# GpSimd's splits in 512 columns, and the state-space output scaled by its root mean square in PSUM

## The chip, the cores and the metric

One core of one Trainium2 chip runs the whole program: one launch, 256 tokens, 32-bit floats in and out. The metric is the device time of one execution in microseconds, as a median over runs. The engines are named as in the profile: PE multiplies matrices (PEld is its loading of weights), DVE is the vector engine, ACT the scalar engine, POOL is GpSimd, SP issues the transfers.

## The reference

Two layers, each an FFN, a mixer and a second FFN, with a root-mean-square norm ahead of and behind each of the three. The first layer's mixer is a hybrid of a convolution and a state-space model, the second's is attention. Only the hybrid is touched here:

```python
def conformer_conv(u, w_dw, b_dw, ln_g, ln_b):
    val, gate = jnp.split(u, 2, axis=-1)
    hid = causal_depthwise_conv(val * jax.nn.sigmoid(gate), w_dw, b_dw)     # 31 taps, 1024 channels
    return jax.nn.silu(layer_norm(hid, ln_g, ln_b))

def mamba2_ssd(z, xbc, dt_raw, ...):
    xbc = jax.nn.silu(causal_depthwise_conv(xbc, conv_w, conv_b))           # 4 taps
    xs, bm, cm = jnp.split(xbc, ...)                                        # 1024, 256, 256 channels
    dt = jax.nn.softplus(dt_raw + dt_bias)
    y = ssd_chunked(xs * dt[..., None], dt * a, bm, cm) + d_skip[:, None] * xs
    y = y.reshape(bsz, seq, 1024) * jax.nn.silu(z)
    return rms_norm(y, norm_g)

def conv_ssd_mixer(u, w_in, ..., w_out):
    conv_in, z, xbc, dt_raw = jnp.split(u @ w_in, [2048, 3072, 4608], axis=-1)
    ya = conformer_conv(conv_in, ...)
    yb = mamba2_ssd(z, xbc, dt_raw, ...)
    return jnp.concatenate([ya, yb], axis=-1) @ w_out
```

`rms_norm` of `yb` multiplies each token's row by one number, `rsqrt(mean(y*y) + 1e-6)`, and each channel by a gain.

## The kernel before

Every product is made in three passes in `f32r`: each operand is the sum of a rounded high part and a low part, and `mm3` adds high x high, high x low and low x high in one PSUM tile. Weights come in units of 1 MB (128 x 2048). `prefetch` loads a unit into a `raw` buffer, ACT copies it to `wh` (the rounding), and then `wl = raw - wh` is made on DVE in pieces of 1024 columns (`PIECE`), or, for the units in `GPSIMD_UNITS`, on POOL in pieces of `POOL_PIECE` columns; ACT copies in the same pieces. There are 4 buffers each of `raw`, `wh` and `wl`, and the loading stands three units ahead of the use.

The units of the hybrid, in the order of use: 33 to 40 the convolution's gate and value columns, 41 and 42 B and C of the state-space model, 43 and 44 its first half of channels (`xbc_pair`), 45 and 46 the first half of the gate z (`gate_z`), 47 and 48 and then 49 and 50 the same for the second half, 51 to 54 the rows of the output projection that meet `yb`, 55 to 58 those that meet `ya`. Everything is recorded through one helper, so that all instructions have line 423, and tile names tell them apart:

- `v`: the four tiles `xs[t][g]` (token tile t of 128 tokens, half g of the channels). They hold x, then x times the skip, then y, then y times silu(z). `y0`, `y1` are the silu(z) of the two token tiles.
- `s<-v,m`, `s<-s,m`, `s<-s,s`, `v<-v,heads`, `v<-v,y` on POOL: x times dt, decays, the skip, the gate.
- `cv`, `t`, `c` on DVE: the 31 taps of the convolution, two chains of additions that end in `cv`; `s<-a,chan,s` and `s<-w,chan,s` are the short convolutions of the state-space part.
- `junk<-v` (ACT) sums squares of y; `m` on DVE adds the halves; `m<-m,mhalf` on POOL is the power -1/2 (`rstd`), and the result for token tile 0 is `m1_13`, for 1 `m1_15`.
- `w<-ident,v` on PE: the transposes of y (`spread`), which ACT and DVE leave as high and low parts in `x` (the tile `ybT`).
- after the last tap: PE transposes the convolution's output, DVE and ACT normalise (`s<-t,m,m`, `s<-s,m,m`), PE transposes back, ACT applies silu (`pt`) and splits into `s` (high), DVE into `s` (low): the operands `yaT` of the last units.
- `a_35`, `a_36` (token tile 0, the two halves of 512 output columns) and `a_37`, `a_38` (token tile 1) are the PSUM tiles in which the output projection is summed: first all of `yb`'s units 51 to 54 for token tile 0, then for 1, then unit 55, then 56 to 58.

What scales y before:

```python
r = self.rstd(ss, EPS)
for g in range(2):
    nc.scalar.activation(xs[t][g], xs[t][g], AF.Copy, scale=r)
```

The order on each engine isn't that of the code: a planner (`schedule`) simulates the recorded operations with a cost for each (`cost`) and hand-over times, and picks for each engine the operation that can start first. A change of a cost or of an operation can thus reorder any engine. Each engine then runs its instructions strictly in that order.

Of the kernel before, what the change touches and what calls it, by code (L numbers as in the profile page):

```python
# [10 lines left out]
F32R = mybir.dt.float32r  # L11
BF16 = mybir.dt.bfloat16
AF = mybir.ActivationFunctionType
# [10 lines left out]
EPS = 1e-6  # L24
# [8 lines left out]
LATE = 800  # L33
PIECE = 1024
FIRST_PIECES = (512, 1024)
POOL_PIECE = 256
ON_POOL = (1, 1, 1)
CONV = 2000
GATE = 200
CONV_INIT = (-500, -100)  # L40
GPSIMD_UNITS = range(38, 56)
SB_BUFS = {"s": 18, "v": 4, "cv": 5, "pt": 4, "sg": 4, "x": 4, "y0": 2, "y1": 2}
PS_BUFS = {"a": 4, "w": 2, "t": 1, "c": 1}
SMALL = {1: 16, 2: 12, 8: 12, 12: 2, 16: 6, 32: 8}
# [391 lines left out]
def cost(op, out):  # L436

    kw = op.kw
    op.table = None
    op.shares_port = False  # L440
    n = out.free_size() if isinstance(out, View) else 0
    if op.engine == "tensor":
        stationary = op.args[1]
        if op.name == "transpose":
            return 109.0, 0.0
        if stationary.ap.dtype == F32R:
            return n / 2.4 + 17.0 if n > 256 else 120.0, 0.0
        return 2 * max(2 * n / 2.4 + 2.5, 112.0), 0.0
    psum = any(isinstance(a, View) and a.buf.kind.psum for a in (*op.args, *kw.values()))
    if op.engine == "scalar":  # L450
        op.table = TABLES.get(op.args[2])
        views = sum(isinstance(kw.get(k), View) for k in ("bias", "scale")) + ("accum_out" in kw)
        return 0.832 * n + (52.0 if psum else 96.0) + 93.0 * views, 0.0
    if op.engine == "gpsimd":
        if op.name == "memset":
            return 100.0, 0.0
        if n == 1:
            return 515.0, 0.0
        return (2.35 if out.ap.dtype == F32R else 1.9) * n + 40.0, 0.0
# [12 lines left out]
    cols = dst.free_size() if isinstance(dst, View) else kw["in_"].free_size()  # L472
    return 475.0, cols * P * 4 / 300.0
# [23 lines left out]
class Kernel:  # L497
# [85 lines left out]
        return r(hi), r(lo)  # L583


    def mm3(self, out, a, b, start, stop):
        mm = self.nc.tensor.matmul
        mm(out, a[0], b[0], start=start, stop=False)
        mm(out, a[0], b[1], start=False, stop=False)
        mm(out, a[1], b[0], start=False, stop=stop)  # L590

    def transposed_tile(self):

# [44 lines left out]
    def acc_pairs(self, acc, lhs, unit, kk, start, stop, halves=(0, 1)):  # L638
        hi, lo = unit
        for hf in halves:  # L640
            c = slice(hf * 512, (hf + 1) * 512)
            self.mm3(acc[hf], lhs, (hi[:, kk, c], lo[:, kk, c]), start, stop)

    def to_transposed(self, src, hi_of, lo_of, n, banks="tc", gain=None):

# [199 lines left out]
    def hybrid(self, xT, done):  # L845
        nc = self.nc
# [13 lines left out]
        dt, a = self.step_sizes(xT)  # L860
# [140 lines left out]
        ybT = self.transposed_tile()  # L1001
        st = [None, None]

        def spread(t):
            self.to_transposed(xs[t], *self.x_out(ybT, t), KB, "ww", gain=chan[:, H_SG : H_SG + KB])

        for t in range(NT):
            if t == 0:
                for g in range(2):
                    lt[1, g] = decays(1, g)  # L1010
            else:
                spread(0)
            ss = self.sm(2)
            for g in range(2):
                hs = slice(8 * g, 8 * g + 8)
                y = xs[t][g]
                py = self.ps([P, 512], "a")
                for hh in range(8):
                    nc.tensor.matmul(py[:, hh * 64 : (hh + 1) * 64], lt[t, g][hh // 4][:, hh % 4, :], xd[t][g][:, hh * 64 : (hh + 1) * 64], start=True, stop=True)
                if t == 0:  # L1020
                    xk = self.slot([P, 512])
                    XK.tensor_tensor(out=heads_view(xk), in0=heads_view(xd[t][g]), in1=by_head(left[:, hs]), op=ALU.mult)
                    pst = self.ps([P, 512], "a")
                    nc.tensor.matmul(pst, b0[:, g, :], xk, start=True, stop=True)
                    st[g] = self.slot([P, 512])
                    nc.scalar.activation(st[g], pst, AF.Copy)
                nc.gpsimd.tensor_tensor(out=heads_view(y), in0=heads_view(y), in1=by_head(self.heads[:, 1, hs]), op=ALU.mult)
                V.tensor_tensor(out=y, in0=y, in1=py, op=ALU.add)
                if t == 1:
                    po = self.ps([P, 512], "a")  # L1030
                    nc.tensor.matmul(po, cT[:, g, P : 2 * P], st[g], start=True, stop=True)
                    V.tensor_tensor(out=heads_view(po), in0=heads_view(po), in1=by_head(grow[:, hs]), op=ALU.mult)
                    V.tensor_tensor(out=y, in0=y, in1=po, op=ALU.add)
                YZ.tensor_tensor(out=y, in0=y, in1=zs[t][g], op=ALU.mult)
                self.sumsq(ss[:, g : g + 1], y, 1 / 32.0)
            r = self.rstd(ss, EPS)
            for g in range(2):
                nc.scalar.activation(xs[t][g], xs[t][g], AF.Copy, scale=r)
        spread(1)


# [28 lines left out]
        def out_unit(src, j, t, unit, start, stop, halves=(0, 1)):  # L1070
            for b in range(2):
                self.acc_pairs(acc[t], src(t, j, b), unit, b, start and b == 0, stop and b == 1, halves)

        for t in range(NT):
            acc[t] = self.acc_tile()
        units = [self.unit(D) for _ in range(4)]
        for t in range(NT):
            for j in range(4):
                out_unit(of_yb, j, t, units[j], j == 0, False)

        unit = self.unit(D)
        for t in range(NT):
            out_unit(of_ya, 0, t, unit, False, False)
        tail = [(j, self.unit(D)) for j in (1, 2, 3)]
        for t in range(NT):
            for j, unit, hf in [(j, unit, hf) for hf in range(2) for j, unit in tail]:
                out_unit(of_ya, j, t, unit, False, j == 3, (hf,))
            done(t, acc[t])

    def load_small(self):  # L1090
# [224 lines left out]
```

## Time and profile before

| | before |
|---|---|
| median of 3 runs | 1132.56 us (1129.19 to 1132.75) |
| profiled execution | 1132.12 us, span 1130.3 us, mean granted clock 0.993 |
| PE busy | 1095.5 us, 97% of the span |
| PEld busy | 919.5 us |
| DVE busy | 738.6 us, 65% |
| ACT busy | 635.2 us, 56% |
| POOL busy | 148.2 us, 13% (200 instructions, nearly all between 205 and 378 us) |

The span runs from the first to the last instruction, and the execution's own time is 1.8 us longer. Times in rows are microseconds from the start of the span. The hybrid lies at about 205 to 397 us. In rows of the timeline, a group stands for several like instructions in a row, and what follows in brackets is how long the engine was idle before it and which engine's work ended that. PEclk is the clock that PE was granted, as a share of full speed.

### The profile page before, as it was taken

To read this page: it belongs to the slowest core of one execution; us is meant where nothing else is said; L and a number is where in the kernel's file an instruction comes from. 1 tells how busy PE (TensorE), PEld (TensorE's weight loads), DVE (VectorE), ACT (ScalarE), POOL (GpSimd) and SP (SyncE) were. 2 spreads that over 40 slices of the span, in tenths; PEclk is the share of its full clock that TensorE was granted. 3 is DMA by queue.
4 is the path that set the end of the run, shared out by engine and by line. 5 is a ranking of instruction groups with operands and counts; after the bars stand their busy time and mean duration, and the time that the engine had idled before them with its cause. 6 is when DMAs were issued, how large, how long until landed. Compare 5 with 4: busy or idle time off the path is not lost.

```text
span 1130.3 us, 15336 instructions
## 1 busy us (share of the span) xinstructions
PE 1095.5 (97%) x5830; PEld 919.5 (81%) x5830; DVE 738.6 (65%) x1248; ACT 635.2 (56%) x1217; POOL 148.2 (13%) x200
## 2 busy tenths in 40 slices
PE   6999999999899999999999999999999999999997
PEld 5888888798767778888878888888877877888885
DVE  5756556799797685655686555667575657555563
ACT  7645545788667564554565454545565456455452
POOL 0000000379795300000010000001000000000000
PEclk9999999999999999999999999999999999999999
DMA  9755454534333466546546546554632424654521
GB/s 349 260 189 186 165 208 149 190 146 150 112 109 116 186 229 217 186 157 215 186 149 224 205 174 221 180 193 159 237 138 79 150 75 152 220 181 174 215 83 38
DMA packets 30203, 196.55 MB, mean 174 GB/s; under 512 B 3633, under 2 KB 4529, under 8 KB 7601
## 3 DMA queue, kind: packets, MB, share of 16 engines
q1 hardware_dynamic: 30128, 195.57, 48.9%
q8 instruction: 45, 0.74, 0.2%
q14 instruction: 30, 0.24, 0.1%
HBM read 194.51 MB, written 1.05 MB: 173 GB/s over the span
## 4 chain that ended last, share of the span: by engine, by line
PE 63%; DVE 4%; ACT 3%; POOL 3%; issue 1%; DVEq 0%; POOLq 0%; ACTq 0%
PE w L423 26%; PE a L423 22%; PE t L423 8%; PE c L423 7%; ACT s L423 1%; POOL wl L423 1%; ACT wh L423 1%; DVE y L423 1%; POOL s L423 1%; DVE wl L423 1%; DVE s L423 1%; POOL m L423 1%; DVE h L423 1%; DVE x L423 0%; DVE m L423 0%
## 5 line engine op out<-in xcount | busy, mean ns | idle before, releaser
L423 DVE TENSOR_TENSOR wl<-raw,wh 128x1024 fp32r<-128x1024 f32 (+1 forms) x322 | 385.1, 1220 | 215.6 <-ACT wh L423 214.0
L423 ACT ACTIVATE wh<-raw 128x1024 fp32r<-128x1024 f32 (+2 forms) x466 | 375.7, 854 | 232.4 <-PE a L423 91.5
L423 PE MATMUL w<-x,wh 128*128 128x512 f32 (+1 forms) x992 | 315.6, 373 | 3.5 <-DVE cv L423 2.1
L423 PE MATMUL w<-x,wl 128*128 128x256 f32 x880 | 247.9, 282 | 0.0
L423 PE MATMUL a<-wh,s 128*128 128x512 f32 x768 | 246.2, 395 | 0.0
L423 PEld LDWEIGHTS w<-x,wh 128*128 128x128 f32 x992 | 179.8, 189 | 40.2 <-DVE cv L423 3.1
L423 PEld LDWEIGHTS a<-wh,s 128*128 128x128 f32 x768 | 143.9, 188 | 34.7 <-DVE s L423 0.6
L423 PEld LDWEIGHTS w<-x,wl 128*128 128x128 f32 x880 | 166.9, 190 | 1.9 <-issue 0.6
L423 PE MATMUL w<-wh,x 128*128 128x512 f32 x480 | 159.3, 405 | 2.5 <-ACT x L423 2.5
L423 PE MATMUL a<-wl,s 128*128 128x512 f32 x384 | 151.8, 395 | 1.8 <-POOL wl L423 1.8
L423 POOL TENSOR_TENSOR m<-m,mhalf 128x1 f32<-128x1 f32 x28 | 19.6, 701 | 939.0 <-DVE m L423 939.0
L423 PEld LDWEIGHTS w<-wh,x 128*128 128x128 f32 x480 | 90.9, 191 | 24.6 <-ACT x L423 3.1
L423 POOL TENSOR_TENSOR wl<-raw,wh 128x256 fp32r<-128x256 f32 x144 | 103.7, 761 | 37.1 <-ACT wh L423 37.0
L423 PE MATMUL t<-x,wh 128*128 128x512 f32 x288 | 102.7, 396 | 0.0
L423 PE MATMUL c<-x,wh 128*128 128x512 f32 x288 | 102.7, 395 | 0.0
L423 PE MATMUL w<-wl,x 128*128 128x512 f32 x240 | 95.5, 400 | 1.7 <-POOL wl L423 1.7
L423 PEld LDWEIGHTS a<-wl,s 128*128 128x128 f32 x384 | 72.1, 188 | 17.6 <-POOL wl L423 2.2
L423 ACT ACTIVATE sg<-w 128x256 f32<-128x256 f32 x96 | 36.6, 382 | 86.7 <-PE w L423 86.6
L423 PE MATMUL t<-x,wl 128*128 128x256 f32 x288 | 80.8, 281 | 0.0
L423 PE MATMUL c<-x,wl 128*128 128x256 f32 x288 | 80.8, 281 | 0.0
L423 DVE TENSOR_TENSOR sg<-w,sg 128x256 f32<-128x256 f32 x72 | 30.3, 421 | 72.6 <-ACT sg L423 72.6
L423 PEld LDWEIGHTS t<-x,wh 128*128 128x128 f32 x288 | 54.0, 188 | 12.8
(167 smaller groups left out, 1211.3 us busy)
## 6 DMA issues: line engine op xcount, KB each, us to landing
raw<-in_weights SPq DMA_DIRECT2D x176, 1024.0 KB, 4.8
g<-in_gains SPq DMA_DIRECT2D x11, 512.0 KB, 4.7
raw<-in_weights SPq DMA_DIRECT2D x4, 256.0 KB, 6.1
raw<-in_weights SPq DMA_DIRECT2D x2, 512.0 KB, 7.9
out<-h SPq DMA_DIRECT2D x4, 256.0 KB, 2.1
s<-in_consts SPq DMA_DIRECT2D x3, 192.0 KB, 4.0
h<-in_x SPq DMA_DIRECT2D x2, 256.0 KB, 2.8
h<-in_x SPq DMA_DIRECT2D x1, 512.0 KB, 6.7
```

What stands on the lines that cost most here:

```text
L423: o.ins = f(*[real(a) for a in o.args], **{k: real(a) for k, a in o.kw.items()})
```

## The change

Four things are changed together.

- The scale by the root mean square leaves `xs` (four ACT instructions on 128x512 in SBUF, ahead of the transposes). `yb`'s products are made with the unscaled y, and as each output row belongs to one token, the sum in PSUM is scaled instead: when `yb`'s products of a token tile are complete, ACT multiplies its two accumulators in place (four ACT instructions on 128x512 in PSUM). `yb`'s products are therefore closed as a group of their own (`stop` at the last), and `ya`'s products are added to the scaled sums.
- `POOL_PIECE` is 512 instead of 256: a unit of POOL is split in 4 pieces instead of 8, and so is ACT's copy of it.
- `GPSIMD_UNITS` ends at 54 instead of 55: unit 55 is split on DVE in two pieces of 1024, and its copy is two ACT instructions.
- The planner's lengths of POOL's instructions are other numbers, by whether an input is broadcast along its last axis.

```diff
-POOL_PIECE = 256
+POOL_PIECE = 512
-GPSIMD_UNITS = range(38, 56)
+GPSIMD_UNITS = range(38, 55)
@@ def cost(op, out):
-        return (2.35 if out.ap.dtype == F32R else 1.9) * n + 40.0, 0.0
+        spread = any(isinstance(v, View) and v.ap.ap[-1][0] == 0 for v in kw.values())
+        return (1.95 if spread else 2.35) * n + (10.0 if spread else 92.0), 0.0
@@ mm3, acc_pairs, out_unit: pass **kw on to the matmuls
@@ hybrid
+        rms = []
...
                 self.sumsq(ss[:, g : g + 1], y, 1 / 32.0)
-            r = self.rstd(ss, EPS)
-            for g in range(2):
-                nc.scalar.activation(xs[t][g], xs[t][g], AF.Copy, scale=r)
+            rms.append(self.rstd(ss, EPS))
         spread(1)
...
         for t in range(NT):
             for j in range(4):
-                out_unit(of_yb, j, t, units[j], j == 0, False)
+                out_unit(of_yb, j, t, units[j], j == 0, j == 3)
+
+            for half in acc[t]:
+                nc.scalar.activation(half, half, AF.Copy, scale=rms[t])
 
         unit = self.unit(D)
         for t in range(NT):
-            out_unit(of_ya, 0, t, unit, False, False)
+            out_unit(of_ya, 0, t, unit, False, False, skip_group_check=True)
```

The instructions of PE are the same ones; their order differs from the second half of the state-space channels on, and from unit 57's copy on every engine's order is the one before. SP's order of transfers is the same throughout. Three places:

On PE, where the low parts of unit 48 (`wl_48`, made on POOL) are first needed. `a_22` is one of the unit's two products, `w_36` and `w_37` are z's, `w_38` is unit 47's. Before:

```order
L423 MATMUL a_22_2945<-x_6_1718,wh_48_2822 128x256 x2
L423 MATMUL a_22_2945<-x_6_1718,wl_48_2860 128x256
L423 MATMUL a_22_2945<-x_6_1718,wh_48_2822 128x256 x2
L423 MATMUL w_36_2828<-wh_46_2581,x_7_1721 128x512
L423 MATMUL a_22_2945<-x_6_1718,wl_48_2860 128x256
```

With the change:

```order
L423 MATMUL a_22_2858<-x_6_1718,wh_48_2738 128x256 x2
L423 MATMUL w_36_2747<-wl_46_2586,x_7_1721 128x512
L423 MATMUL w_36_2747<-wh_46_2516,x_7_1721 128x512
L423 MATMUL w_37_2885<-wh_45_2433,x_4_1710 128x512
L423 MATMUL w_37_2885<-wl_45_2520,x_4_1710 128x512
L423 MATMUL w_37_2885<-wh_45_2433,x_4_1710 128x512 x2
L423 MATMUL w_38_2895<-x_4_1710,wh_47_2661 128x256 x2
```

Two products of `w_36`, four of `w_37` and all 24 of `w_38` now stand ahead of the first product of `x_6` with `wl_48` (the row after the last one shown is the next of `w_38`); before, that product followed at once, and one of `w_36` stood ahead of the second.

On PE, where y of token tile 0 is transposed (`w_44` from `v_0`, `w_45` from `v_2`), ahead of the first products of unit 51. Before:

```order
L423 MATMUL w_43_3435<-ident_0_70,cv_14_2853 128x128 x2
L423 MATMUL w_41_3223<-wh_50_3064,x_7_1721 128x512
L423 MATMUL w_44_3466<-ident_0_70,v_0_2891 128x128 x4
L423 MATMUL w_45_3476<-ident_0_70,v_2_3184 128x128 x4
L423 MATMUL a_35_3489<-wh_51_3138,x_8_3482 128x512
```

With the change:

```order
L423 MATMUL w_44_3307<-ident_0_70,v_0_2807 128x128 x4
L423 MATMUL w_41_3246<-wh_50_3001,x_7_1721 128x512
L423 MATMUL w_41_3246<-wl_50_3013,x_7_1721 128x512
L423 MATMUL w_41_3246<-wh_50_3001,x_7_1721 128x512 x2
L423 MATMUL w_41_3246<-wl_50_3013,x_7_1721 128x512
L423 MATMUL w_41_3246<-wh_50_3001,x_7_1721 128x512
L423 MATMUL a_35_3330<-wh_51_3036,x_8_3318 128x512
L423 MATMUL a_35_3330<-wl_51_3071,x_8_3318 128x512
L423 MATMUL a_36_3336<-wh_51_3036,x_8_3318 128x512
L423 MATMUL a_36_3336<-wl_51_3071,x_8_3318 128x512
L423 MATMUL a_35_3330<-wh_51_3036,x_8_3318 128x512
L423 MATMUL w_45_3349<-ident_0_70,v_2_3081 128x128 x4
```

The transposes of `v_0` have moved ahead of the last six products of z (`w_41`), and those of `v_2` from ahead of unit 51's first products to behind five of them.

On ACT, between `yb`'s transposes and the operands of `ya`. `s_61` is the first normalised half of the convolution, `pt` its silu. Before:

```order
L423 ACTIVATE x_11_3506<-w_47_3532,chan_0_115 128x128 x2
L423 ACTIVATE wh_54_3564<-raw_54_3351 128x256 x8
L423 ACTIVATE s_61_3663<-s_47_3426,m1_17_3657,m1_16_3641 128x512
```

With the change:

```order
L423 ACTIVATE wh_54_3347<-raw_54_3074 128x512
L423 ACTIVATE a_35_3330<-a_35_3330,m1_13_3359 128x512
L423 ACTIVATE a_36_3336<-a_36_3336,m1_13_3359 128x512
L423 ACTIVATE wh_55_3505<-raw_55_3259 128x1024 x2
L423 ACTIVATE wh_56_3545<-raw_56_3339 128x1024 x2
L423 ACTIVATE s_61_3567<-s_47_3278,m1_17_3555,m1_16_3533 128x512
```

The scaling of token tile 0 and the copies of units 55 and 56, which stood behind the chain of `s_61`, now stand ahead of it.

More of the change, by code (lines that the diff above doesn't have):

```diff
@@ L583, in unit, with mm3 @@
         return r(hi), r(lo)
-    def mm3(self, out, a, b, start, stop):
+    def mm3(self, out, a, b, start, stop, **kw):
         mm = self.nc.tensor.matmul
-        mm(out, a[0], b[0], start=start, stop=False)
-        mm(out, a[0], b[1], start=False, stop=False)
-        mm(out, a[1], b[0], start=False, stop=stop)
+        mm(out, a[0], b[0], start=start, stop=False, **kw)
+        mm(out, a[0], b[1], start=False, stop=False, **kw)
+        mm(out, a[1], b[0], start=False, stop=stop, **kw)
     def transposed_tile(self):
@@ L636, in by_parts, with acc_pairs @@
             nc.vector.scalar_tensor_tensor(out=out, in0=ps[:, 0, :], scalar=scale, in1=out, op0=ALU.mult, op1=ALU.add)
-    def acc_pairs(self, acc, lhs, unit, kk, start, stop, halves=(0, 1)):
+    def acc_pairs(self, acc, lhs, unit, kk, start, stop, halves=(0, 1), **kw):
         hi, lo = unit
@@ L641, in acc_pairs @@
             c = slice(hf * 512, (hf + 1) * 512)
-            self.mm3(acc[hf], lhs, (hi[:, kk, c], lo[:, kk, c]), start, stop)
+            self.mm3(acc[hf], lhs, (hi[:, kk, c], lo[:, kk, c]), start, stop, **kw)
     def to_transposed(self, src, hi_of, lo_of, n, banks="tc", gain=None):
@@ L1068, in hybrid, with out_unit @@
         of_ya = lambda t, j, b: tuple(part[j][:, t, b, :] for part in yaT)
-        def out_unit(src, j, t, unit, start, stop, halves=(0, 1)):
+        def out_unit(src, j, t, unit, start, stop, halves=(0, 1), **kw):
             for b in range(2):
-                self.acc_pairs(acc[t], src(t, j, b), unit, b, start and b == 0, stop and b == 1, halves)
+                self.acc_pairs(acc[t], src(t, j, b), unit, b, start and b == 0, stop and b == 1, halves, **kw)
         for t in range(NT):
@@ L1086, in hybrid @@
             for j, unit, hf in [(j, unit, hf) for hf in range(2) for j, unit in tail]:
-                out_unit(of_ya, j, t, unit, False, j == 3, (hf,))
+                out_unit(of_ya, j, t, unit, False, j == 3, (hf,), skip_group_check=True)
             done(t, acc[t])
```

## Prediction

> **What bounds the kernel now.** I read the page's busy times first, then PE's waits in the hybrid, then the granted clock in short windows around the long ones, and last the timelines of the engines that PE waits for.
>
> ```profile
> PE 1095.5 (97%) x5830; PEld 919.5 (81%) x5830; DVE 738.6 (65%) x1248; ACT 635.2 (56%) x1217; POOL 148.2 (13%) x200
> ```
>
> PE is the bound: 34.8 us of the span (1130.3 - 1095.5) are all that it is not busy. A gain must come from PE's idle time or from a low clock. The list of PE's waits, window 200 to 420 us (waiting for, total, times, longest):
>
> ```profile
> PE a L423 <- POOL wl L423: 4.6, 2, 2.8
> PE w L423 <- ACT v L423: 2.4, 1, 2.4
> PE w L423 <- POOL wl L423: 1.7, 1, 1.7
> PE a L423 <- POOL s L423: 0.8, 1, 0.8
> PE w L423 <- ACT wh L423: 0.3, 1, 0.3
> ```
>
> These are 9.8 us of waits for what the change touches: POOL's splits and POOL's other work, and the scaling by the root mean square. PE's timeline places them:
>
> ```profile
> 295.77 0.49 PE L423 MATMUL a<-x,wl 128*128 128x256 f32 x1 [2.81 <-POOL wl L423]
> 325.96 1.12 PE L423 MATMUL a<-s,pt 128*128 128x512 f32 x2 [0.78 <-POOL s L423]
> 333.00 0.50 PE L423 MATMUL w<-wl,x 128*128 128x512 f32 x1 [1.65 <-POOL wl L423]
> 343.12 1.30 PE L423 MATMUL w<-ident,v 128*128 128x128 f32 x6 [2.41 <-ACT v L423]
> 375.87 0.50 PE L423 MATMUL a<-wl,s 128*128 128x512 f32 x1 [1.80 <-POOL wl L423]
> ```
>
> I call them A (unit 48's low part), C (POOL's decay), D (unit 49's low part), E (the transposes of y) and F (unit 55's low part). The windows behind A, D, E and F (us, PE, PEld, DVE, ACT, POOL, PEclk, DMA share, GB/s):
>
> ```profile
> core 0: us, PE busy (x) PEld busy (x) DVE busy (x) ACT busy (x) POOL busy (x), PEclk, DMA share, GB/s
> 295.70:299.00 3.30, 3.23 (x11) 2.90 (x12) 0.00 (x0) 0.74 (x2) 1.39 (x3) 0.53 0.22 70
> 333.00:336.00 3.00, 3.00 (x13) 2.45 (x14) 3.00 (x9) 0.00 (x0) 3.00 (x5) 1.00 0.81 328
> 343.10:347.30 4.20, 4.18 (x15) 3.31 (x16) 4.05 (x14) 4.20 (x13) 3.02 (x5) 0.59 0.01 2
> 375.80:379.00 3.20, 3.13 (x14) 2.56 (x15) 3.20 (x3) 0.00 (x0) 0.01 (x1) 1.00 0.66 220
> ```
>
> After the waits of 2.81 and 2.41 us PE was granted about half its clock, after 1.65 and 1.80 us the full one. So A cost another 3.3 x (1 - 0.53) = 1.55 us and E 4.2 x (1 - 0.59) = 1.72 us. What the change can win at most: A 4.36, the wait for a copy 0.30, C 0.78, D 1.65, E 4.13, F 1.80, together 13.0 us.
>
> **The change, part by part.**
>
> *The pieces.* Prices on POOL, as forms with min/median/max ns:
>
> ```profile
> L423 POOL TENSOR_TENSOR wl<-raw,wh x129: 712/737/1728, 229.3 to 374.1; 128x256 fp32r<-128x256 f32 x129
> L423 POOL TENSOR_TENSOR v<-v,y x4: 1282/1303/1312, 323.6 to 342.3; 128x512 f32<-128x512 f32 x4
> L423 POOL TENSOR_TENSOR v<-v,heads x4: 1032/1044/1077, 293.0 to 325.8; 128x512 f32<-128x512 f32 x4
> ```
>
> and POOL's timeline at A and behind it:
>
> ```profile
> 295.00 2.09 POOL L423 TENSOR_TENSOR wl<-raw,wh 128x256 fp32r<-128x256 f32 x3
> 302.81 9.83 POOL L423 TENSOR_TENSOR wl<-raw,wh 128x256 fp32r<-128x256 f32 x14 [5.72 <-ACT wh L423]
> ```
>
> Fourteen pieces of 256 took 9.83 us, 0.70 each. A piece of 512 isn't in the trace. Two of 256 make 1.40; the nearest row, another subtraction-like instruction with two full inputs and 512 columns, is 1.30 (the 1.04 row has a broadcast input). I take 1.30 to 1.40, and 1.40 for the sum: POOL then does the same work in the same time, up to 0.1 x 56 pieces faster (units 41 to 54), which only adds margin. ACT's copies come in half as many instructions, on an engine that is 56% busy: nothing.
>
> *A* doesn't need a faster POOL. The first piece behind POOL's four other instructions ends at 295.00 + 0.70 = 295.7 now. With pieces of 512, two rather than two and a half stand ahead of those four and one behind, the same sum of columns: 295.7 again. But PE now has 6 products of 512 columns and 24 of 256 ahead of that need. Their pace from PE's timeline (12 products between the last two rows, 18 between the first two):
>
> ```profile
> 299.87 0.39 PE L423 MATMUL w<-x,wh 128*128 128x256 f32 x2
> 301.90 0.64 PE L423 MATMUL w<-wh,x 128*128 128x512 f32 x2
> 304.71 0.39 PE L423 MATMUL w<-wh,x 128*128 128x512 f32 x1
> ```
>
> 2.81 / 12 = 0.234 and 2.03 / 18 = 0.113, so 6 x 0.234 + 24 x 0.113 = 4.1 us. PE came to A at 295.77 - 2.81 = 292.96 - about 0.4 for the product at its side = 292.6; it needs the piece at 296.7, 1 us after it is there. A goes, clock and all: 4.36.
>
> *C and D.* POOL's order puts unit 49's four pieces ahead of unit 50's; before, two of them stood last. D goes: 1.65. C's decay comes as POOL gets to it; all that precedes it is there 4 us earlier with A, and POOL is at most as late as PE: I take 0.78, ends 0 and 0.78. The 0.30 likewise.
>
> *E, the scaling.* What stood in the way, on POOL and then ACT:
>
> ```profile
> 338.44 1.30 POOL L423 TENSOR_TENSOR v<-v,y 128x512 f32<-128x512 f32 x1
> 339.68 2.12 POOL L423 TENSOR_TENSOR wl<-raw,wh 128x256 fp32r<-128x256 f32 x3
> 341.75 0.56 POOL L423 TENSOR_TENSOR m<-m,mhalf 128x1 f32<-128x1 f32 x1
> 340.71 0.57 ACT L423 ACTIVATE s<-w 128x512 f32<-128x512 f32 x1
> 342.34 1.33 ACT L423 ACTIVATE v<-v,m 128x512 f32<-128x512 f32 x2
> ```
>
> `v_2` got its gate at 338.44 to 339.7; then the sum of squares, three pieces of a split on POOL, the power (341.75), and the scale on ACT (342.34) had to end before the first transpose at 343.12. Now the transposes need only y. `v_0`'s gate ran at 323.6 (the first of the row above), long before. `v_2`'s is needed six products of z, the transposes of `v_0` and five products of unit 51 later than `v_0`'s. E goes, clock and all: 4.13. The removed four ACT instructions (1.33 for two) are off the path then; the four added ones work on PSUM in place, which no row shows; the copies `v<-a` out of PSUM of that size give the nearest:
>
> ```profile
> L423 ACT ACTIVATE v<-a x4: 579/581/590, 287.0 to 313.8; 128x512 f32<-128x512 f32 x4
> ```
>
> 0.58 each. Token tile 0's pair lies beside the 48 products of `yb` for token tile 1 (48 x 0.234 = 11 us), 1's pair beside unit 55's 12 products for token tile 0 (2.8 us): nothing on the path as long as ACT gets to it. POOL's powers move with it: no engine waits for them but ACT's scaling, up to 10 us later.
>
> *F and the chain of `ya`.* Unit 55 leaves POOL, two DVE pieces replace eight:
>
> ```profile
> 367.25 8.56 POOL L423 TENSOR_TENSOR wl<-raw,wh 128x256 fp32r<-128x256 f32 x8 [8.55 <-ACT wh L423]
> L423 DVE TENSOR_TENSOR wl<-raw,wh x9: 1211/1225/1757, 370.3 to 394.4; 128x1024 fp32r<-128x1024 f32 x9
> ```
>
> POOL had to wait 8.55 us for the copy, because that stood on ACT behind `ya`'s chain; now it stands ahead of it and DVE needs 2 x 1.22. F goes: 1.80. But whether PE can start `ya` 11 us earlier hangs on the convolution:
>
> ```profile
> 299.45 0.48 DVE L423 SCALAR_TENSOR_TENSOR s<-a,chan,s 128x255 f32<-128x255 f32 x1 [4.09 <-ACT s L423]
> 354.42 0.48 DVE L423 SCALAR_TENSOR_TENSOR cv<-cv,chan,c 128x256 f32<-128x256 f32 x1
> 359.19 1.60 ACT L423 ACTIVATE s<-s,m,m 128x512 f32<-128x512 f32 x2 [6.02 <-DVE m L423]
> 364.61 0.73 ACT L423 ACTIVATE s<-pt 128x256 fp32r<-128x256 f32 x2
> L423 ACT ACTIVATE wh<-raw 128x1024 fp32r<-128x1024 f32 x13 | 12.9, 1064 | 7.5 <-DMA raw<-in_weights 5.7 <-PE w L423 1.2 <-PE a L423 0.6
> 365.07 0.76 DVE L423 TENSOR_TENSOR s<-pt,s 128x256 fp32r<-128x256 f32 x2 [0.76 <-ACT s L423]
> 371.56 0.40 PE L423 MATMUL a<-wh,s 128*128 128x512 f32 x1
> ```
>
> The last tap ended at 354.9, ACT normalised from 359.19 (4.3 later), `ya`'s first high part was there at 365.0 (5.8 after that), and PE came to it only at 371.56. So there are 6.5 us of slack. Without A to E PE comes earlier by 4.36 + 0.30 + 0.78 + 1.65 + 4.13 = 11.2, at 360.3. The taps move too: DVE's 4.09 at 299.45 is A's (that ACT instruction reads `a_22`), and its shorter waits behind PE go with it; 4.1 to 5.6 us, the taps end at 349.3 to 350.8, ACT could normalise at 353.6 to 355.1. There the copies of units 55 and 56 now stand ahead, and unit 56's needs the buffer that PE frees with unit 52's last product of token tile 1, about 24 products and 16 small transposes before 360.3, so at some 353; with two copies of 1.06 (mean of the row) it ends at 355. `ya`'s first part is there at 355 + 5.8 = 360.8 to 361. PE waits about 0.6. Everything behind on ACT (token tile 1's scaling, units 57 and 58) shifts with that.
>
> *The sum.* 13.0 - 0.6 for `ya`. Unit 54's last piece on POOL ends by my count about when PE needs it (15 pieces and 5 other instructions behind C), and PE has 6 to 12 products of token tile 1 to fill with: 0 to 1, taken as 0.5. Small waits for a PSUM buffer at changed places: 0.4. Net 11.5. From unit 57 on the orders are as before and PE is nearly always busy, so the gain stays to the end. 1132.1 - 11.5 = 1120.6; the profiled execution is 0.4 under the median, so by the median it would be 1121.0. I say 1121.
>
> **The rivals.**
>
> *The convolution holds `ya`.* If the taps' end doesn't move (DVE, 65% busy overall, fills the holes with other work), `ya` still starts at about 365.2: PE wins 6.4 there and F's 1.8, and waits 5 us with some 1.6 of low clock behind it: 6.6 gained, 1125.9. Half the move gives 1123.5. For it: the slack of 6.5 is less than the 11.2 that PE gains. Against: DVE's 4.09 is plainly a wait for A.
>
> *E stays in part.* The transposes also need one of two PSUM buffers `w`, and the one before was copied out by ACT at 340.71 to 341.3, so that without the scaling alone E would still be 0.6 us, and with copies of z's gate and unit 53 between, up to 2, with the low clock: 13.0 - 1.5 - 3 = 8.5 gained, 1124.
>
> *Slower: long pieces on POOL stretch.* The maximum of the split's row is 1.728 for 256 columns, at 370 to 376, when DVE split too and its pieces took up to 1.757 instead of 1.22: both slow down together. If DVE's taps did that to pieces of 512, each would cost more than 1.40, and POOL is without a pause from unit 41 to A and nearly so from 303 to 346. With all 56 pieces on PE's path, the 13 us are eaten up at 1.40 + 13 / 56 = 1.63 a piece, and at 1.73 it is 18.5 - 13 = 5.5 slower: 1138. Against: the median of 129 such pieces is 0.737 beside the same taps. The Trainium skill, "SBUF — State Buffer", section "Who interferes with whom", says that a DVE instruction with two SBUF inputs contends with a GpSimd instruction that reads SBUF; the trace agrees at 370 to 376 and shows nothing of it for the taps.
>
> *The clock isn't A's and E's.* Low clock at 295.7 and 343.1 could be set by something else than the wait, and stay: 13.0 - 3.3 - 1.5 = 8.2, 1124.3. Against: the four windows show half the clock behind the two longer waits and all of it behind the two shorter. The Trainium skill, "TensorE: Matmul & The Clock Gate", section "HAM oscillation — how this bites in real kernels", gives idle gaps above about 3.4 us as what costs the clock; by that 2.81 and 2.41 would be too short, and the sum would be this rival's. The trace shows half the clock right behind both.
>
> *The change doesn't bring it about.* PE's order fits the planner's times, not the chip's, and the waits come back elsewhere: 1129.5 to 1135.
>
> **How the numbers follow.** Forecast (1118 to 1123) 0.52; the convolution 0.20; E in part 0.08; the clock 0.04; POOL's pieces 0.09, of it 0.05 slower and 0.04 within 0.3%; no effect 0.07. 0.3% (3.4 us) is about what a measurement of this kernel can tell from none: faster 0.84, same 0.11, slower 0.05. The low end is the whole 13.0 and 2 us of other waits of the window with it, 1117; the high end takes in the convolution's rival and a little, 1128.
>
> **What would show it.** In the profile of the changed kernel: POOL's pieces of 512 at 1.25 to 1.45; no wait of PE for POOL `wl` over 1 us and none for ACT `v`; PEclk 1.00 from 275 to 350; DVE's 4.09 gone; `a<-a,m` on ACT at 0.5 to 0.7; `ya`'s first product at 360 to 362. It would be wrong if PE waits several us for `s` (the convolution) or for `wl` of units 50 to 54 (POOL).

## The result and the profile after

| | before | with the change |
|---|---|---|
| median, first comparison | 1131.97 us (1129.19 to 1132.75) | 1116.22 us (1115.59 to 1119.84) |
| median, second comparison | 1131.86 us (1129.57 to 1132.82) | 1118.12 us (1115.83 to 1119.13) |
| span of the profiled execution | 1130.3 us | 1114.2 us, in the second 1116.3 us |

The ratio is 0.9872 (95% interval 0.9844 to 0.9899), in the second comparison 0.9877 (0.9861 to 0.9893): some 14 us faster, where 11.5 were forecast. Of the measured medians the second stands at the low end of the range (1117 to 1128), the first 0.8 us below it. The mean granted clock of a single execution was 0.992 to 0.995 in every recorded run of the kernel before, and 0.997 to 0.999 in every run of the changed one. The page of the changed kernel:

```profile
PE 1089.9 (98%) x5830; PEld 915.7 (82%) x5830; DVE 738.4 (66%) x1250; ACT 629.3 (56%) x1143; POOL 131.4 (12%) x124
```

PE's waits, window 200 to 420 us, the whole list (waiting for, total, times, longest):

```profile
PE w L423 <- DVE pt L423: 0.7, 1, 0.7
PE w L423 <- DVE s L423: 0.5, 2, 0.3
PE c L423 <- DVE pt L423: 0.3, 1, 0.3
PE t L423 <- DVE y L423: 0.2, 1, 0.2
PE a L423 <- ACT s L423: 0.2, 1, 0.2
PE a L423 <- ACT v L423: 0.2, 1, 0.2
```

None of the five rows shown of before is left: no wait for POOL, none for the scaled y (ACT `v` here is the wait of 0.2 that was there before, too), none for a copy. The windows in which PE's clock had dropped (columns as in the prediction):

```profile
275.00:300.00 25.00, 24.68 (x168) 21.80 (x167) 23.91 (x62) 18.14 (x39) 20.42 (x18) 1.00 0.38 127
325.00:350.00 25.00, 24.93 (x124) 20.09 (x124) 22.42 (x65) 15.07 (x37) 19.11 (x17) 1.00 0.50 169
```

Full clock. The prices that were not in the trace, and the chain of `ya`:

```profile
L423 POOL TENSOR_TENSOR wl<-raw,wh x59: 1265/1298/1346, 229.6 to 343.7; 128x512 fp32r<-128x512 f32 x59
290.81 2.55 POOL L423 TENSOR_TENSOR wl<-raw,wh 128x512 fp32r<-128x512 f32 x2
L423 ACT ACTIVATE a<-a,m x4: 662/666/677, 345.4 to 362.1; 128x512 f32<-128x512 f32 x4
348.02 0.48 DVE L423 SCALAR_TENSOR_TENSOR cv<-cv,chan,c 128x256 f32<-128x256 f32 x1
351.86 2.01 ACT L423 ACTIVATE wh<-raw 128x1024 fp32r<-128x1024 f32 x2 [1.62 <-PE a L423]
353.77 1.51 ACT L423 ACTIVATE s<-s,m,m 128x512 f32<-128x512 f32 x2
359.88 0.50 PE L423 MATMUL a<-wh,s 128*128 128x512 f32 x1 [0.20 <-ACT s L423]
```

A piece of 512 takes 1.27 (two in 2.55). The last tap ends at 348.5 instead of 354.9, ACT normalises as soon as unit 56's copy is through, and `ya`'s first product comes at 359.88 instead of 371.56.

Where the 16.1 us between the two profiled spans are, by the same PE instruction in both traces: 0.9 at the start (the transposes of token tile 1 at 15.23 instead of 16.11), 12.7 in the hybrid (between the two products that stood at 279.6 and 400.0 us before), 0.5 spread thinly over the FFNs, 0.9 in attention, 1.1 behind PE's last product, in the transfer out. In the second profile the hybrid gives 12.7 again, but the start 0.1, and attention is 0.6 slower than before: what lies outside the hybrid belongs in good part to the single execution. Most of the start is clock: PE has its full clock from 14.5 us on instead of 16.0 (15.5 in the second profile). The part in attention is clock, too: the same wait of 2.1 us stands in both traces, with 4 us behind it at a clock of 0.57 before and 1.00 after:

```profile
872.19 0.50 PE L423 MATMUL w<-x,wh 128*128 128x512 f32 x1 [2.14 <-DVE cv L423]
872.20:876.20 4.00, 4.00 (x14) 3.38 (x15) 1.49 (x2) 1.65 (x3) 0.00 (x0) 0.57 0.05 8
```

```profile
858.19 0.50 PE L423 MATMUL w<-x,wh 128*128 128x512 f32 x1 [2.12 <-DVE cv L423]
858.20:862.20 4.00, 4.00 (x23) 3.53 (x24) 1.49 (x2) 2.69 (x5) 0.00 (x0) 1.00 0.11 18
```

### The profile page after: what moved, and what is told of

Its sections match the earlier page's. It is cut to its first block, busy times and chain, and to the rows that moved or that the text cites. A ratio compares the mean times of both kernels' runs of the same rounds, so it can differ in the third digit from the quotient of the medians.

```text
span 1114.2 us, 15190 instructions
## 1 busy us (share of the span) xinstructions
PE 1089.9 (98%) x5830; PEld 915.7 (82%) x5830; DVE 738.4 (66%) x1250; ACT 629.3 (56%) x1143; POOL 131.4 (12%) x124
## 4 chain that ended last, share of the span: by engine, by line
PE 85%; DVE 8%; ACT 4%; issue 1%; POOL 1%; DMA 1%; SPq 0%; DVEq 0%; POOLq 0%; ACTq 0%
PE w L423 35%; PE a L423 30%; PE t L423 10%; PE c L423 10%; DVE c L423 1%; ACT wh L423 1%; DVE wl L423 1%; DVE y L423 1%; DVE t L423 1%; ACT s L423 1%; DVE s L423 1%; POOL m L423 1%; DVE h L423 1%; DVE x L423 1%; DVE m L423 1%
## 5 line engine op out<-in xcount | busy, mean ns | idle before, releaser
L423 ACT ACTIVATE wh<-raw 128x1024 fp32r<-128x1024 f32 (+1 forms) x392 | 368.8, 978 | 228.3 <-PE a L423 93.8
L423 POOL TENSOR_TENSOR wl<-raw,wh 128x512 fp32r<-128x512 f32 x68 | 85.7, 1299 | 25.0 <-ACT wh L423 24.0
L423 PEld LDWEIGHTS c<-x,wh 128*128 128x128 f32 x288 | 54.0, 188 | 12.7
```

The costliest lines, as they stand in the source:

```text
L423: o.ins = f(*[real(a) for a in o.args], **{k: real(a) for k, a in o.kw.items()})
```

## The experiments

Ratios are to the kernel before, of the runs on the same chip.

### The scaling alone

The change to `hybrid`, `mm3`, `acc_pairs` and `out_unit` is kept; the three other parts are undone:

```diff
-POOL_PIECE = 512
+POOL_PIECE = 256
-GPSIMD_UNITS = range(38, 55)
+GPSIMD_UNITS = range(38, 56)
-        spread = any(...)
-        return (1.95 if spread else 2.35) * n + (10.0 if spread else 92.0), 0.0
+        return (2.35 if out.ap.dtype == F32R else 1.9) * n + 40.0, 0.0
```

> Only the scaling moves to PSUM; pieces of 256, unit 55 on GpSimd, the planner's old lengths. Theory (each of the waits A, C, D, E, F has its own cause): only E goes. PE's order ahead of y's transposes is the one before, so A (2.81 and half the clock behind it), C and D stay; at E at most 0.6 us is left, until ACT has copied out the PSUM buffer that the transposes need, and full clock behind it: 3 to 4 us faster, 1128 to 1129. F stays within 1 us, since unit 55's copy is still behind the chain of ya on ACT. Rival (the PSUM buffer holds the transposes too): E keeps over 1.5 us and its low clock, less than 1.5 us faster.

Measured: 1123.36 us, ratio 0.9925 (0.9905 to 0.9945), 8.5 us faster. From PE's waits and the stretch behind A:

```profile
PE a L423 <- POOL wl L423: 2.8, 1, 2.8
PE w L423 <- POOL wl L423: 1.7, 1, 1.7
PE w L423 <- ACT s L423: 0.7, 1, 0.7
```

```profile
295.01 0.39 PE L423 MATMUL a<-x,wl 128*128 128x256 f32 x1 [2.78 <-POOL wl L423]
295.00:299.00 4.00, 3.99 (x29) 3.80 (x30) 1.57 (x5) 1.16 (x2) 1.33 (x2) 1.00 0.34 111
```

By its waits the theory holds for A, C, D and E: E is gone but for 0.7 us until ACT has emptied the PSUM buffer (the rival's mechanism, at the theory's size), the others stand as they were. But the time moved by twice as much as expected. F, which was to stay, is gone as well: the freed ACT copies the first two pieces of unit 55 ahead of `ya`'s chain. And the wait of 2.78 at A cost no clock this time, though its length is that of before, where PE had 0.53 (the section "What a wait costs in clock" shows why). E with its clock 3.4, F 1.8 and A's clock 1.6 make 6.8; between the same two products as above the hybrid is 6.1 shorter. The rest of the 8.5 lies outside it.

### The change without the move of the scaling

```diff
-            rms.append(self.rstd(ss, EPS))
+            r = self.rstd(ss, EPS)
+            for g in range(2):
+                nc.scalar.activation(xs[t][g], xs[t][g], AF.Copy, scale=r)
-            for half in acc[t]:
-                nc.scalar.activation(half, half, AF.Copy, scale=rms[t])
```

> The change without the move of the scaling: y is still scaled in SBUF by ACT ahead of its transposes; everything else as changed. Theory: A, C, D and F stay gone and E is back, with a wait of PE for ACT v of 2 to 3 us and half the clock behind it: 1119.5 to 1121, 3.5 to 4.5 slower than the changed kernel. Rival (the shorter queue on GpSimd alone had made E harmless): E under 1 us, within 1.5 us of the changed kernel.

Measured: 1120.74 us, ratio 0.9905 (0.9891 to 0.9920), 3.7 us more than the changed kernel's 0.9872. Waits and clock:

```profile
PE w L423 <- ACT v L423: 3.4, 1, 3.4
325.00:350.00 25.00, 21.63 (x102) 17.33 (x101) 22.58 (x65) 15.48 (x37) 20.00 (x18) 0.93 0.45 168
```

E is back and is the only long wait. What it costs, 3.2 us (by the change's second ratio) to 3.9 (in the hybrid of the two profiles), is near the forecast's term of 4.13. The wait is longer than before (2.4), since PE comes earlier to it.

### The change with the planner's old lengths

```diff
-        spread = any(...)
-        return (1.95 if spread else 2.35) * n + (10.0 if spread else 92.0), 0.0
+        return (2.35 if out.ap.dtype == F32R else 1.9) * n + 40.0, 0.0
```

> The change with the planner's old lengths of GpSimd's instructions. PE's order then has unit 48's low part needed at once, as before the change, and GpSimd's has two pieces of unit 49 behind unit 51's. Theory (it is the order that took A and D away, not the faster pieces): PE waits 1 to 3 us at A and 1 to 4 at D again; 4 to 8 us slower than the changed kernel, 1120 to 1124. Rival (GpSimd's pieces of 512 took A and D away, by 0.1 us a piece or 3 us from unit 41 to A): under 1 us at A, within 2 us of the changed kernel.

Measured: 1119.50 us, ratio 0.9894 (0.9879 to 0.9909), 2.5 us more than the change by its first ratio and 1.9 by its second; the intervals overlap. The longest wait is

```profile
PE w L423 <- ACT y L423: 0.9, 1, 0.9
```

There is no wait at A or D, though PE needs unit 48's low part at once, as before. So my theory falls: PE's new order isn't needed. That faster pieces alone are enough isn't shown by it, though, since the order of GpSimd changed with them:

```profile
277.47 11.30 POOL L423 TENSOR_TENSOR wl<-raw,wh 128x512 fp32r<-128x512 f32 x9
288.71 2.08 POOL L423 TENSOR_TENSOR s<-v,m 128x512 f32<-128x512 f32 x2
298.53 2.55 POOL L423 TENSOR_TENSOR wl<-raw,wh 128x512 fp32r<-128x512 f32 x2 [5.74 <-ACT wh L423]
```

All pieces of unit 48 now stand ahead of GpSimd's four other instructions; before, three of 256 stood behind them (295.00), 4 us later for it. An estimate: before, GpSimd came to the four at 290.99 with five of unit 48's eight pieces done, here at 288.71 with all, and the three pieces are 2.1 us; so the price alone would have brought some 4.4 us where PE had waited 2.8.

### The change with pieces of 256

```diff
-POOL_PIECE = 512
+POOL_PIECE = 256
```

> The change with pieces of 256 on GpSimd (14 units, 112 pieces) and the planner's new lengths. The order has unit 47's products ahead of unit 48's low part, but one piece of unit 49 behind unit 51's. Theory of the order: no wait at A, a wait of 1 to 3 us at D, 2 to 4 us slower than the changed kernel, 1118 to 1120. Rival (the pieces' price, 2 x 0.70 against 1.27, 0.13 us x 56 = 7 us on PE's path): 6 us or more slower, with waits for wl at A and at units 50 to 54.

Measured: 1119.78 us, ratio 0.9895 (0.9880 to 0.9910), 2.6 us more than the change.

```profile
PE w L423 <- POOL wl L423: 3.3, 1, 3.3
```

No wait at A with the old price and the new order; D (3.3) is there as expected, with a low clock behind it (0.93 from 325 to 350). The 2.6 us (2.0 by the second ratio) are what the theory said, but not the whole of what the wait costs: in the hybrid of this profile 5.4 us are lost, and part of them comes back outside. So A goes with the old price in the new order, and with the new price in PE's old order; with both, POOL is at unit 48's second half at 290.81 + 1.27 = 292.1, over 3 us before the 295.7 that the prediction counted with.

### Pieces, lengths and unit 55, each alone

```diff
-POOL_PIECE = 256
+POOL_PIECE = 512
```

> Only the pieces on GpSimd are 512 columns; scaling in SBUF, unit 55 on GpSimd (4 pieces), the planner's old lengths, by which PE needs unit 48's low part at once, as before. Theory (a piece of 512 at 1.26 against 2 x 0.70 brings GpSimd to unit 48's second half 3 to 4 us earlier, and that alone takes A away): no wait at A, E still there (2 to 3.5 us, ACT v), F between 0 and 1.8: 5 to 7 us faster, 1125 to 1127. Rival (A needs the new order): A over 1.5 us, less than 3 us faster.

Measured: 1124.96 us, ratio 0.9938 (0.9923 to 0.9953). A and D are gone; E took over much of it, with a low clock behind it (0.86 from 325 to 350):

```profile
PE w L423 <- ACT v L423: 5.8, 1, 5.8
PE a L423 <- POOL wl L423: 0.3, 1, 0.3
```

PE comes to y's transposes 7.5 us earlier, the scaling only 4.2: E grows by the difference. As in the run with the old lengths, GpSimd's order changed with the pieces.

The planner's lengths alone:

```diff
-        return (2.35 if out.ap.dtype == F32R else 1.9) * n + 40.0, 0.0
+        spread = any(...)
+        return (1.95 if spread else 2.35) * n + (10.0 if spread else 92.0), 0.0
```

> Only the planner's lengths are new; pieces of 256, scaling in SBUF, unit 55 on GpSimd. PE's order has unit 47's products ahead of unit 48's low part, and GpSimd's leaves unit 49's last piece behind unit 51's. Theory: A goes (4.4 with its clock), D grows from 1.65 to about 3.3, E and F stay: 1 to 4 us faster, 1128 to 1130.5. Rival (the order alone makes the change): 8 us or more faster.

Measured: 1126.98 us, ratio 0.9958 (0.9944 to 0.9973); waits 3.3 at D, 2.5 at E, 1.3 at F, none at A, as the theory had it, with half the clock behind D and E (0.80 from 325 to 350); 4.7 us faster where 1 to 4 were expected. In the hybrid of the profile only 1.6 are won; the rest lies outside it.

Unit 55 alone:

```diff
-GPSIMD_UNITS = range(38, 56)
+GPSIMD_UNITS = range(38, 55)
```

> Only unit 55 moves from GpSimd to DVE, in two pieces; its copy still stands on ACT behind the chain of ya, and PE's order is the one before, row for row. Theory: DVE ends the split earlier than GpSimd's eight pieces did (two of 1.22 against 8 x 0.70 and the stretch to 1.73), so F falls from 1.8 to 0.5 or less: 1 to 2 us faster, 1129.5 to 1131. Rival (the two copies of 1.06 delay the first piece as much): F as before, within 1 us.

Measured: 1125.04 us, ratio 0.9939 (0.9925 to 0.9954), 6.9 us. F is gone; A (2.8) and E (2.4), with the low clock behind them, and D (1.6) stand. The waits thus explain 1.8 to 2.1 us. In the profiled spans another 1.3 is at the start, 1.1 behind PE's last product, and some 2 us spread over the FFNs behind the hybrid, 0.1 to 0.5 in each 300 products, with PE's order unchanged. The gain is 4 to 5 us larger than the waits show. What it comes from stays open; unit 55 need not be the cause, for these FFNs (400 to 758 us before) are 0.2 to 2.1 us shorter than in the one profile of before in every other run here, too.

What each part is worth in the hybrid alone, between the same two products of the profiles (us, one execution each, in which one drop of the clock more or less makes 1.7):

| | alone, against before | taken out of the change |
|---|---|---|
| scaling in PSUM | 6.1 | 3.9 |
| pieces of 512 | 3.9 | 5.4 |
| the planner's lengths | 1.6 | 1.7 |
| unit 55 on DVE | 2.1 | not run |

Together they give 12.7; the four parts nearly add up.

### Is there slack in the convolution's chain?

Twelve DVE instructions at the end of the taps, put into the changed kernel and the kernel before. The planner counts them as nothing. In the changed kernel every engine's order stays; in the kernel before PE's doesn't, nine more products of `yb` come ahead of the transposes of the last taps:

```diff
+        for _ in range(3):
+            for k in range(4, 8):
+                V.tensor_scalar(hid[k], hid[k], 1.0, None, ALU.mult)
+                nc.ops[-1].cost = 0.0
         ln_half(1, "tc")
```

> The changed kernel with the convolution's end made late: twelve more DVE instructions (each of the four last tiles, 128x256, times 1.0, three times over), some 0.25 to 0.3 us each, 3.0 to 3.6 us in all; the order is otherwise that of the changed kernel. Theory (with the change nothing is left between the end of ya's chain and PE): PE waits for ya's operands 2.5 to 4 us, and the time goes up by 2.5 to 4 us, more if the clock falls. Rival (there is slack as before): within 1 us of the changed kernel.

> The kernel before with the same twelve DVE instructions ahead of the convolution's transposes. Theory (PE came 6.5 us after ya's operands): 3.0 to 3.6 us of it are used up, yet unit 55 on GpSimd moves with the chain, so the wait F grows from 1.8 to some 5; 0 to 3.5 us slower, with no wait for ya's own operands. Rival (the chain was the bound before, too): PE waits for s.

Measured: with the change 1121.67 us, ratio 0.9911 (0.9897 to 0.9926), 4.4 us more than the change by the first ratio, 3.8 by the second; the kernel before with the twelve 1134.38 us, ratio 1.0026 (1.0014 to 1.0038), 2 to 3 us slower. The twelve, their wait on PE and the clock behind it, in the changed kernel:

```profile
L423 DVE TENSOR_SCALAR cv<-cv x12: 293/294/296, 347.8 to 352.6; 128x256 f32<-128x256 f32 x12
PE t L423 <- DVE cv L423: 2.8, 3, 1.5
350.00:375.00 25.00, 22.87 (x100) 17.73 (x101) 19.62 (x37) 17.03 (x29) 2.09 (x2) 0.93 0.32 115
```

and in the kernel before:

```profile
PE t L423 <- DVE cv L423: 2.2, 3, 0.9
PE a L423 <- POOL wl L423: 5.5, 3, 2.8
```

PE doesn't wait at `ya`'s operands, where I had looked, but ten microseconds earlier, at the transposes of the last taps (`t<-cv`). The slack there can be read from the two kernels without the twelve. PE in the kernel before, then in the changed one:

```profile
355.02 0.49 PE L423 MATMUL t<-ident,cv 128*128 128x128 f32 x3
355.58 0.27 PE L423 MATMUL t<-ident,cv 128*128 128x128 f32 x1
348.49 0.49 PE L423 MATMUL t<-ident,cv 128*128 128x128 f32 x3
348.93 0.27 PE L423 MATMUL t<-ident,cv 128*128 128x128 f32 x1
```

The last tap ends at 354.42 + 0.48 = 354.90 before and at 348.02 + 0.48 = 348.50 with the change, and the fourth of these transposes begins at 355.58 and 348.93: 0.7 and 0.4 us later. In the changed kernel the twelve put the end of the taps off by 4.4 us (to 352.89), more than their own 3.5, and 2.8 of it became waiting. So the theory has the size right for the changed kernel, at another place than it named. For the kernel before its premise falls: there was as little slack, 0.7 us and not 6.5; the rival's wait for `s` didn't come either. In the kernel before F grew, too, to 2.7 in two pieces (5.5 less A's 2.8). In that profile the hybrid is 6.9 us longer, more than the medians show: with the waits came half clock from 358 and 378 us on, while A cost none.

### Pieces of 1024

```diff
-POOL_PIECE = 512
+POOL_PIECE = 1024
```

> The changed kernel with pieces of 1024 on GpSimd (28 instead of 56). Price: 0.70 for 256 and 1.26 for 512 make 0.56 per 256 columns and 0.14 for an instruction, so 2.38 for 1024; GpSimd saves another 4 us. Theory (in the changed kernel PE no longer waits for GpSimd, so its speed is worth nothing more): no gain; and as the planner now puts token tile 1's scaling ahead of the chain of ya on ACT, that chain begins only when PE has ended yb, and PE waits up to 6 us: 0 to 7 us slower than the changed kernel. Rival (GpSimd's price still counts): 2 us or more faster.

Measured: 1127.94 us, ratio 0.9963 (0.9950 to 0.9975), 10 us slower than the change. POOL's price, and DVE at the end of the taps with the wait that follows:

```profile
L423 POOL TENSOR_TENSOR wl<-raw,wh x34: 2372/2416/2439, 220.2 to 342.1; 128x1024 fp32r<-128x1024 f32 x34
354.11 0.48 DVE L423 SCALAR_TENSOR_TENSOR cv<-cv,chan,t 128x256 f32<-128x256 f32 x1
354.50 2.36 DVE L423 TENSOR_TENSOR wl<-raw,wh 128x1024 fp32r<-128x1024 f32 x2
356.77 0.47 DVE L423 SCALAR_TENSOR_TENSOR cv<-cv,chan,c 128x256 f32<-128x256 f32 x1
357.32 2.36 DVE L423 TENSOR_TENSOR wl<-raw,wh 128x1024 fp32r<-128x1024 f32 x2
PE w L423 <- DVE s L423: 4.4, 1, 4.4
```

The price is what the line through 256 and 512 gives (2.38 expected), and PE waits for no split any more. What costs is the order that the planner makes of it: six splits of units 55 to 57 (two of them at 351.83, not shown) stand ahead of and between the last four taps, which end at 360.5 instead of 348.5, and PE waits for the normalised convolution, with a clock of 0.74 from 350 to 375. That PE waits for GpSimd's splits neither here nor in the changed kernel speaks for the theory that faster pieces are worth nothing from 512 on; the new order hides what they would be worth alone. The place of the loss was another one than I named.

### What a wait costs in clock

A program of bursts of 128x512 products and waits between them, nothing of the reference (`BURSTS` are 30 to 52 products, `STEPS` 1 to 11):

```diff
+        for n, steps in zip(BURSTS, STEPS):
+            ...
+            for k in range(n):
+                nc.tensor.matmul(a, s, wide, start=k == 0, stop=k == n - 1)
+            ...
+            nc.vector.scalar_tensor_tensor(out=d[:, 0:P], in0=a[:, 0:P], scalar=0.0, in1=base, op0=ALU.mult, op1=ALU.add)
+            for _ in range(steps - 1):
+                nc.vector.tensor_scalar(d[:, 0:P], d[:, 0:P], 1.0, None, ALU.mult)
+            ...
+            nc.vector.tensor_scalar(s, d[:, 0:P], 1.0, None, ALU.mult)
```

> Another program: nothing of the reference is computed. 66 bursts of 30 to 52 matmuls of 128x512, and between them PE waits for a chain of 2 to 12 dependent DVE instructions on 128x128, so that waits of about 0.8 to 4 us are spread over the time. It asks what a wait costs in clock. Theory of the prediction (a wait of 2.4 us or more halves the clock): all waits over 2.4 us are followed by some 3 us of half clock, none under 1.8. Rival 1 (only gaps over about 3.4 us do it): none below 3.4. Rival 2 (chance, by where the wait falls): between 1.8 and 3.4 us some do and some don't, the more the longer.

Two waits of the same length and the 4 us behind each, twice:

```profile
465.37 1.86 PE L423 MATMUL a<-wide,s 128*128 128x512 f32 x7 [2.04 <-DVE s L423]
465.40:469.40 4.00, 4.00 (x18) 3.29 (x19) 0.00 (x0) 0.00 (x0) 0.00 (x0) 1.00 0.00 0
735.77 1.39 PE L423 MATMUL a<-wide,s 128*128 128x512 f32 x5 [2.04 <-DVE s L423]
735.80:739.80 4.00, 4.00 (x12) 3.17 (x13) 0.00 (x0) 0.00 (x0) 0.00 (x0) 0.67 0.00 0
254.28 1.39 PE L423 MATMUL a<-wide,s 128*128 128x512 f32 x5 [3.35 <-DVE s L423]
254.30:258.30 4.00, 4.00 (x18) 3.29 (x19) 0.00 (x0) 0.00 (x0) 0.00 (x0) 1.00 0.02 4
518.98 1.62 PE L423 MATMUL a<-wide,s 128*128 128x512 f32 x3 [3.35 <-DVE s L423]
518.70:522.70 4.00, 3.73 (x10) 3.00 (x11) 0.13 (x1) 0.00 (x0) 0.00 (x0) 0.58 0.02 4
```

Counted over all waits of the trace:

| wait, us | up to 1.78 | 2.04 | 2.31 | 2.57 | 2.83 | 3.09 | 3.35 |
|---|---|---|---|---|---|---|---|
| waits | 30 | 6 | 6 | 5 | 6 | 6 | 6 |
| with low clock behind | 0 | 3 | 4 | 4 | 4 | 4 | 3 |

The theory falls and so does rival 1. Rival 2 has it right that some do and some don't; with five or six waits of a length, whether the longer ones do it more often can't be told. But within an execution it isn't chance. The trace records when the clock changes: the half clock lasts 3.413 us (two such stretches on end in two of the 22 cases), and every stretch begins on one grid of 3.413 us, to within 0.001 us. The window in which the wait ahead of 735.77 lies, and the next one on the grid:

```profile
733.72:737.13 3.41, 1.37 (x7) 1.17 (x7) 1.65 (x7) 0.00 (x0) 0.00 (x0) 1.00 0.00 0
737.13:740.54 3.41, 3.41 (x10) 2.63 (x9) 0.00 (x0) 0.00 (x0) 0.00 (x0) 0.50 0.00 0
```

All 22 waits with low clock behind them had 2.04 us or more in one window of the grid, and the next window had half clock; the other 43 had at most 1.93 in any. Of the four waits above, the one ahead of 465.37 is cut by the grid into 0.74 and 1.31, that ahead of 254.28 into 1.52 and 1.84; the one ahead of 735.77 lies in one window, and 518.98 has 3.06 in one. The long waits of the kernels fit, with the limit at about 1.9 (1.89 did it once, 1.93 once didn't): A lay whole in one window before, and in the run of the scaling alone the grid cuts it into 1.85 and 0.93; the wait of 2.1 us in attention lay whole in one window before, and is cut into 1.52 and 0.60 with the change. Where the grid stands differs from execution to execution. Each stretch costs PE half of 3.413, 1.7 us. The Trainium skill, "TensorE: Matmul & The Clock Gate", section "What's actually happening", has a window of 3413 ns that runs freely and doesn't start with the kernel; the trace agrees, with 3.413 us. Its rule in "HAM oscillation — how this bites in real kernels", that gaps over about 3.4 us do it, doesn't hold here: 2.04 is enough in 3 of 6.

### The changed kernel again

> The changed kernel once more, beside the same runs of the kernel before. Theory (behind a wait of 2 us or more the clock is halved or not by chance, so that single executions of either kernel differ by multiples of 1.7 us): the same waits as in the first profile within 0.3 us, 1115 to 1119 in single runs, and the wait of 2.1 us near 858, which cost no clock in the first profile, may cost it here. Rival (the clock goes with the program): the same low stretches as in the first profile.

Measured: 1118.12 us, ratio 0.9877 (0.9861 to 0.9893), single runs 1115.83 to 1119.13. The list of waits up to 420 us is the one above within 0.2 us. The wait near 858 cost no clock again: the grid of this execution cuts it into 1.87 and 0.25. So the clock goes neither by chance at the wait nor with the program, but with the grid. The profile has half clock from 886 on, which the first hasn't, with only 0.6 us of waits in the window ahead of it, among small products of attention; what set that one off isn't shown.

## Why the prediction was right, and where not

- **A, C, D, E, F go.** All five did, with the clock. In the hybrid 12.7 us were won, against 11.5 forecast and 13.0 at most: of the 1.5 taken off, `ya`'s wait is 0.2 rather than 0.6, and the 0.9 for unit 54 and for PSUM buffers didn't come.
- **The price of a piece.** 1.27, below my bounds of 1.30 to 1.40: the row I leaned on gives 1.30 as the length of one instruction, and its successor starts earlier than that. The step "A doesn't need a faster POOL" is right (pieces of 256 with the new order have no A). Pieces of 512 take A away with PE's old order, too, but there GpSimd's order had changed.
- **E.** The removal of the scaling alone leaves 0.7 us, as the rival "E stays in part" priced it (0.6); with the order of the whole change nothing is left.
- **The scaling in PSUM** takes 0.67 an instruction, not 0.58, and lies beside products: no engine waits for it.
- **Long pieces don't stretch** beside the taps. The rival that ended slower needed 1.63 us a piece; the longest of 59 took 1.35, beside the same taps. Beside DVE's own splits they do: in the run of the pieces alone, with unit 55 still on GpSimd, two pieces of 512 took 2.27 and 2.35 us from 366.5 on, and DVE's pieces of 1024 beside them 2.3 instead of 1.2.
- **The convolution.** The step "6.5 us of slack" looked at the wrong place: at the transposes of the last taps, which PE needs first, 0.7 us were left. The rival built on it didn't occur because the taps did move, by 6.4 us, of which 0.9 is the earlier start; 4.1 to 5.6 were expected. Had they not, PE would have waited at the transposes, by an estimate some 10 us (11.2 less 0.7) and not the 5 that the rival priced.
- **The clock.** I took half clock as what a wait of over 2 us costs. It costs that only where 1.9 to 2 us of the wait fall into one window of the grid. The 1.55 and 1.72 in the sum were right for that profiled execution, by how its grid stood, and the wait A without them stands in the run of the scaling alone; in this the sum had luck.
- **The size.** The 3.4 us outside the hybrid (start, attention's clock, FFNs, end) had no term. Attention's 0.9 and most of the start are the clock, and the second profile hasn't got them. The run with unit 55 alone shows that not everything outside the hybrid is chance: its four executions lie within 0.9 us of each other, and 4 to 5 us of its 6.9 are at no wait of the profiled one; the cause is open.

## What to carry to other kernels

Where a norm's factor belongs to rows of a product, it can be applied to the sum instead of the operand, and what it buys is the wait for the factor, not the instructions. Before a wait is priced, look at who would be late next: the faster pieces alone made the wait for the scaling grow from 2.4 to 5.8 us, which took back part of what they had won. A single profile can be off by 1.7 us for each wait of 2 to 3 us, by where the clock's grid happens to stand. And a planner orders by its own lengths: a piece size that is better on its engine (1024) cost 10 us by where the other engines' work was put.

## What the hardware showed

Behind a wait of 2.04 to 3.35 us PE's clock was halved in 22 of 35 cases, for 3.41 us (6.83 in two), or not at all; behind 30 waits of up to 1.78 us never. What decided was how much of the wait lay in one window of a grid of 3.41 us: in that program 2.04 us and more always did it, 1.93 and less never. GpSimd's subtraction of 128 partitions took 0.70, 1.27 and 2.4 us for 256, 512 and 1024 columns with both inputs full, so some 0.13 us an instruction beside 0.0022 a column. Two such subtractions, on GpSimd and DVE at once, slowed each other: GpSimd's 256 columns from 0.74 to 1.7 us, DVE's 1024 from 1.2 to between 1.6 and 1.8.
